# The first two tiles loaded over both DMA queues, split by even and odd partitions

## The chip, the cores and the metric

The kernel runs on one core of a Trainium2 chip. The metric is the device time of one execution, in microseconds. The kernel before was timed in 3 runs, and one further execution was profiled.

## The reference

A gated linear unit on a float32 matrix of 8192 x 8192: the left half of the columns times the sigmoid of the right half. The output is 8192 x 4096.

```python
def reference(x: np.ndarray) -> np.ndarray:
    a, b = np.split(x, 2, axis=-1)
    return a * (1 / (1 + np.exp(-b)))
```

268.4 MB are read and 134.2 MB are written.

## The kernel before

The rows are cut into 32 tiles of 256 rows. A tile has two rows in each of the 128 partitions (`R = 2`), so a partition's share is one run of 64 KiB of the input, its row 0 and its row 1 one behind the other, and 32 KiB of the output. Neighbouring partitions are 128 KiB apart in the input (`h=2` in the rearrangement: two tiles interleave).

There are two input buffers (`xs`, `SLOTS = 2`) and two output buffers (`os`); tile i uses buffer i mod 2. In a tile the columns are counted in eighths, 0 to 4 for the first row and 4 to 8 for the second.

All loads are issued by SyncE (`load`, line 63), all stores by ScalarE (`store`, line 68). Each of the two engines has a DMA queue of its own; on the page the sync queue is q1 and the scalar queue q10. A queue's transfers follow one another, and both queues feed the same 16 DMA engines, which take packets from either. A packet here is one partition's contiguous piece.

The work on a tile (`work`) is: ScalarE takes the sigmoid of the right columns in place (line 92), then VectorE multiplies by the left columns into the output buffer (line 97). In tiles 1 to 30 the sigmoid is one instruction over the tile, and the product is cut into the first 3/16 of the columns (`few`, on GpSimd from tile 2 on, on VectorE in tile 1) and the rest on VectorE. A no-operation on TensorE (line 87) joins the wait for the tile's load and for the store that empties the output buffer. Tiles 0 and 31 are worked in four pieces (`fourths`), each a sigmoid of 128 x 2048 and a product.

Tile 0 is loaded as its two rows, in two transfers, and stored as its two rows; every other load is one transfer of the whole tile, every other store but the last tile's too.

The order is written out at the end of `_tiles`: loads 0 and 1 first; then for each tile its work, the load of tile i + 2 (which waits for the products of tile i, the last readers of that input buffer), and its store. Each instruction keeps its place in the program on its engine. The only waits are those that `place` is given; the others are declared needless because they follow from the ones that are kept.

`_launch_early` takes SyncE's first load out of the body and puts it into the entry block, ahead of the barrier that starts the body, so that it is issued at time 0. `_close_on_sync` rewrites the end: GpSimd clears the semaphores, and SyncE waits for the last store.

Of the kernel before, what the change touches and what calls it, by code (L numbers as in the profile page):

```python
# [8 lines left out]
def _tiles(ctx, tc, x, out):  # L9
    nc = tc.nc  # L10
    P = nc.NUM_PARTITIONS
    DEP = mybir.DependencyInfo(mybir.DependencyClass.Sync, mybir.DependencyReason.DATA)
    fp32 = mybir.dt.float32
    SIG = mybir.ActivationFunctionType.Sigmoid

    n_rows, n_cols = x.shape
    half = n_cols // 2
    R = 2
    SLOTS = 2
    n_tiles = n_rows // (P * R)  # L20
    x_g = x.rearrange("(g p h r) m -> g h p (r m)", p=P, h=2, r=R)
    out_g = out.rearrange("(g p h r) m -> g h p (r m)", p=P, h=2, r=R)

    pool = ctx.enter_context(tc.tile_pool(name="io", bufs=1))
    xs = [pool.tile([P, R * n_cols], fp32, name=f"x_sb{k}") for k in range(SLOTS)]
    os = [pool.tile([P, R * half], fp32, name=f"o_sb{k}") for k in range(SLOTS)]

    whole = [(0, 8)]
    rows = [(0, 4), (4, 8)]
    cut = half // 16 * 3  # L30
    few_and_most = [(0, 8, 0, cut), (0, 8, cut, half)]
    fourths = [(k, k + 2, k % 4 * half // 4, (k % 4 + 2) * half // 4) for k in range(0, 8, 2)]
    loads = [whole] * n_tiles
    works = [few_and_most] * n_tiles
    stores = [whole] * n_tiles
    behind = [0] * n_tiles
    loads[0] = stores[0] = rows
    works[0] = works[-1] = fourths
    stores[-1] = [(0, 4), (4, 6), (6, 8)]
    behind[-1] = 1  # L40

    def meet(a, b):
        return a[0] < b[1] and b[0] < a[1]

    traced = [[] for _ in range(SLOTS)]
    load_of, mul_of, store_of = {}, {}, {}

    def place(i, ins, *needs):


        kept = {n.ins.name for n in needs}
        for e in traced[i % SLOTS]:
            if e.ins.name not in kept:
                tc.declare_no_dep(ins.ins, e.ins, reason="follows from the waits that are kept")
        traced[i % SLOTS].append(ins)
        tc.keep_in_program_order(ins)
        return ins

    def load(i):
        for lo, hi in loads[i]:  # L60
            c = slice(lo * n_cols // 4, hi * n_cols // 4)
            free = [m for w, m in mul_of.get(i - SLOTS, []) if meet(w, (lo, hi))]
            ins = nc.sync.dma_start(out=xs[i % SLOTS][:, c], in_=x_g[i // 2, i % 2, :, c])  # L63
            load_of.setdefault(i, []).append(((lo, hi), place(i, ins, *free)))

    def store(i, lo, hi):
        c = slice(lo * half // 4, hi * half // 4)
        ins = nc.scalar.dma_start(out=out_g[i // 2, i % 2, :, c], in_=os[i % SLOTS][:, c])  # L68
        done = [m for w, m in mul_of[i] if meet(w, (lo, hi))]
        store_of.setdefault(i, []).append(((lo, hi), place(i, ins, *done)))  # L70

    def work(i, lo, hi, near, far):

        rows = xs[i % SLOTS].rearrange("p (r h m) -> p r h m", r=R, h=2)
        packed = os[i % SLOTS].rearrange("p (r m) -> p r m", r=R)
        r, c = slice(lo // 4, (hi + 3) // 4), slice(near, far)
        b = rows[:, r, 1, c]
        landed = [s for w, s in load_of[i] if meet(w, (lo, hi))]
        gone = [s for w, s in store_of.get(i - SLOTS, []) if meet(w, (lo, hi))]
        middle = 0 < i < n_tiles - 1  # L80
        rest = middle and near
        if rest:
            before = mul_of[i].pop()[1]
        else:
            g = rows[:, r, 1, :] if middle else b
            if middle and gone:
                met = nc.tensor.nop(nofuse=True)  # L87
                for n in (*landed, *gone):
                    tc.add_manual_dep(met.ins, n.ins.name, DEP, reason="joins the waits")
                place(i, met, *landed, *gone)  # L90
                landed = [met]
            before = nc.scalar.activation(out=g, in_=g, func=SIG)  # L92
            for n in landed:
                tc.add_manual_dep(before.ins, n.ins.name, DEP, reason="both have landed")
            place(i, before, *landed)
        engine = nc.gpsimd if far == cut and i > 1 else nc.vector
        mul = engine.tensor_mul(out=packed[:, r, c], in0=rows[:, r, 0, c], in1=b)  # L97
        tc.add_manual_dep(mul.ins, before.ins.name, DEP, reason="follows the gate, or the first columns")
        place(i, mul, before, *(() if middle else gone))
        mul_of.setdefault(i, []).append(((lo, hi), mul))  # L100

    for i in range(SLOTS):
        load(i)
    for i in range(n_tiles):
        due = list(stores[i])
        for k, piece in enumerate(works[i]):
            work(i, *piece)
            ready = works[i][k - behind[i]][1] if k >= behind[i] else 0
            while len(stores[i]) > 1 and k < len(works[i]) - 1 and due[0][1] <= ready:
                store(i, *due.pop(0))  # L110
        if i + SLOTS < n_tiles:
            load(i + SLOTS)
        for lo, hi in due:
            store(i, lo, hi)
# [71 lines left out]
@with_exitstack  # L186
def kernel(
    ctx: ExitStack,
    tc: tile.TileContext,
    x: bass.AP,  # L190
    out: bass.AP,
):
    nc = tc.nc
    with ExitStack() as pools:
        _tiles(pools, tc, x, out)
    tc.close()
    tc.compile()
    _launch_early(nc)
    _close_on_sync(nc)
# [30 lines left out]
```

## Time and profile before

| | us |
|---|---|
| median of 3 runs (lowest, highest) | 932.75 (932.47, 932.77) |
| the profiled execution | 932.44 |
| its span, first to last instruction | 931.1 |
| VectorE busy | 232.5 |
| ScalarE busy | 227.0 |
| GpSimd busy | 99.3 |

402.67 MB pass through the 16 DMA engines at a mean of 432 GB/s. The loads take 66.6% of these engines' time, the stores 33.4%. The page's chain of work that ended last is, by share of the span, DMA 69%, VectorE 12%, ScalarE 12% and GpSimd 5%.

How to read these: the span is counted within the profiled execution; what lies around it, 1.34 us, belongs to the time and not to the span. An engine's busy time counts what it computes, not the issuing of DMAs. A row of the timeline or of the chain gives a start and a length in us from the span's start. "ACTq" and "SPq" are the sequencers of ScalarE and SyncE, which issue DMAs. The DMA row of the page gives the mean busy share of the 16 DMA engines in each fortieth of the span, in tenths. "L97" is line 97 of the kernel.

### The profile page before, as it was taken

The numbers are of one execution on the slowest core, as the hardware profiler recorded it, in microseconds if no ns is written. First come the engines' busy times: TensorE is split into PE (matmuls) and PEld (weight loads), VectorE is DVE, ScalarE is ACT, GpSimd is POOL, SyncE is SP. The second block draws the span as 40 slices with busy tenths as digits, with TensorE's granted clock in tenths as the row PEclk, the third lists the DMA queues.
The fourth block names the chain that finished last, engine by engine and source line by source line (L and its number), as shares of the span: only waits on it lengthen the run. The fifth ranks groups of instructions, "written<-read, shape, count | busy, mean of one in ns | idle before, by whom it ended". The sixth has DMA issues, their size and how long they took to land.

```text
span 931.1 us, 299 instructions
## 1 busy us (share of the span) xinstructions
DVE 232.5 (25%) x39; ACT 227.0 (24%) x39; POOL 99.3 (11%) x33
## 2 busy tenths in 40 slices
DVE  1133203332023320233302333023330233311333
ACT  2123332033320333202332023320233202333023
POOL 0001110111101111011110111101111011110110
DMA  9999999999999999999999999999999999999998
GB/s 405 450 442 414 428 450 425 453 405 428 450 428 450 410 469 405 428 450 428 450 405 459 420 428 451 425 450 408 431 448 428 450 408 467 408 428 450 427 452 383
DMA packets 9793, 402.67 MB, mean 432 GB/s; under 512 B 1088, under 2 KB 1088, under 8 KB 1088
## 3 DMA queue, kind: packets, MB, share of 16 engines
q1 hardware_dynamic: 4752, 268.44, 66.6%
q10 hardware_dynamic: 5040, 134.22, 33.4%
q14 instruction: 1, 0.01, 0.0%
HBM read 268.44 MB, written 134.22 MB: 432 GB/s over the span
## 4 chain that ended last, share of the span: by engine, by line
DMA 69%; DVE 12%; ACT 12%; POOL 5%; issue 0%; PEldq 0%; ACTq 0%; SPq 0%
DMA out_dram<-o_sb 60%; DVE o_sb L97 12%; ACT x_sb L92 12%; DMA x_sb<-in_x_dram 9%; POOL o_sb L97 5%; PEldq L87 0%; ACTq L68 0%; SPq L63 0%
## 5 line engine op out<-in xcount | busy, mean ns | idle before, releaser
L97 DVE TENSOR_TENSOR o_sb<-x_sb 128x6656 f32<-128x6656 f32 (+2 forms) x39 | 232.5, 5969 | 690.3 <-POOL o_sb L97 632.7
L92 ACT ACTIVATE x_sb<-x_sb 128x8192 f32<-128x8192 f32 (+1 forms) x38 | 225.7, 5949 | 692.7 <-PEq L87 632.9
L97 POOL TENSOR_TENSOR o_sb<-x_sb 128x1536 f32<-128x1536 f32 x29 | 99.1, 3417 | 793.9 <-ACT x_sb L92 793.9
L92 ACT ACT_TABLE_LOAD x1 | 1.3, 1283 | 0.8 <-PEq L214 0.8
L214 POOL MEMSET const-float32-0.0<- 128x1 f32 x1 | 0.1, 99 | 0.2 <-issue 0.2
L214 POOL MEMSET const-bfloat16-1.0<- 128x1 bf16 x1 | 0.1, 103 | 0.0
L214 POOL MEMSET const-uint8-127<- 128x1 uint8 x1 | 0.1, 103 | 0.0
L214 POOL MEMSET const-float32-1.0<- 128x1 f32 x1 | 0.1, 99 | 0.0
## 6 DMA issues: line engine op xcount, KB each, us to landing
out_dram<-o_sb ACTq DMA_DIRECT2D x30, 4096.0 KB, 40.2
x_sb<-in_x_dram SPq DMA_DIRECT2D x2, 4096.0 KB, 16.6
out_dram<-o_sb ACTq DMA_DIRECT2D x3, 2048.0 KB, 27.8
out_dram<-o_sb ACTq DMA_DIRECT2D x2, 1024.0 KB, 8.3
x_sb<-in_x_dram SPq DMA_DIRECT2D x31, 40.0
```

The lines of the kernel that those rows point to most:

```text
L92: before = nc.scalar.activation(out=g, in_=g, func=SIG)
L97: mul = engine.tensor_mul(out=packed[:, r, c], in0=rows[:, r, 0, c], in1=b)
L214: nc = _bacc.Bacc("TRN2", target_bir_lowering=False, num_devices=1)
```

## The change

Loads 0 and 1 are each split into two transfers: the even partitions on the sync queue, the odd partitions on the scalar queue, each with the partition's whole 64 KiB run. Tile 0 is no longer loaded row by row, and its output is stored in one transfer behind its last product, on the scalar queue. The later loads, the work and all other stores are as before. `by_row` is defined and not used.

```diff
     whole = [(0, 8)]
-    rows = [(0, 4), (4, 8)]
...
-    loads = [whole] * n_tiles
+    every, even, odd = slice(0, P), slice(0, P, 2), slice(1, P, 2)
+    by_parity = [(nc.sync, (0, 8), even), (nc.scalar, (0, 8), odd)]
+    by_row = [(nc.sync, (0, 4), every), (nc.scalar, (4, 8), every)]
+    first_loads = [by_parity, by_parity]
     works = [few_and_most] * n_tiles
     stores = [whole] * n_tiles
     behind = [0] * n_tiles
-    loads[0] = stores[0] = rows
     works[0] = works[-1] = fourths
...
+    def load_over_both(i):
+        for k, (engine, (lo, hi), p) in enumerate(first_loads[i]):
+            c = slice(lo * n_cols // 4, hi * n_cols // 4)
+            ins = engine.dma_start(out=xs[i][p, c], in_=x_g[i // 2, i % 2, p, c])
+            load_of.setdefault(i, []).append(((lo, hi), place(i, ins)))
+
     def load(i):
-        for lo, hi in loads[i]:
-            c = slice(lo * n_cols // 4, hi * n_cols // 4)
-            free = [m for w, m in mul_of.get(i - SLOTS, []) if meet(w, (lo, hi))]
-            ins = nc.sync.dma_start(out=xs[i % SLOTS][:, c], in_=x_g[i // 2, i % 2, :, c])
-            load_of.setdefault(i, []).append(((lo, hi), place(i, ins, *free)))
+        c = slice(0, R * n_cols)
+        free = [m for _, m in mul_of[i - SLOTS]]
+        ins = nc.sync.dma_start(out=xs[i % SLOTS][:, c], in_=x_g[i // 2, i % 2, :, c])
+        load_of.setdefault(i, []).append(((0, 8), place(i, ins, *free)))
...
     for i in range(SLOTS):
-        load(i)
+        load_over_both(i)
```

## The prediction

> **What bounds the kernel now.** I read the page's head, its DMA parts, the windows by stage, the chain that ended last, and the timeline of the first 70 us.
>
> From the page: the span, the DMA busy tenths, the queues (packets, MB, share of 16 engines' time).
>
> ```profile
> span 931.1 us, 299 instructions
> DMA  9999999999999999999999999999999999999998
> q1 hardware_dynamic: 4752, 268.44, 66.6%
> q10 hardware_dynamic: 5040, 134.22, 33.4%
> ```
>
> The windows (stretch, its length, busy time of DVE, ACT, POOL, clock, DMA share, GB/s):
>
> ```profile
> 0.00:46.20 46.20, 8.98 (x4) 8.70 (x5) 0.21 (x4) 1.00 1.02 431
> 99.60:871.60 772.00, 191.47 (x27) 189.78 (x27) 92.26 (x27) 1.00 1.00 434
> ```
>
> The 16 DMA engines have no idle stretch: the loads of the sync queue (q1) and the stores of the scalar queue (q10) add up to 100.0% of their time, and the first 46 us run at 431 GB/s beside 434 in the steady state. VectorE and ScalarE are busy a quarter of it. So only two things change the time: bytes moved more slowly, or engines left without work.
>
> The chain (start, length, what), at both ends of its regular part:
>
> ```profile
> 1.15 45.06 DMA x_sb<-in_x_dram
> 46.23 7.04 ACT x_sb L92
> ...
> 117.35 40.23 DMA out_dram<-o_sb
> ...
> 813.60 40.21 DMA out_dram<-o_sb
> ```
>
> Between 117.35 and 813.60 lie 12 rounds of two tiles: 29.01 us a tile. 32 tiles at that pace are 928.3 us, and the span is 931.1. All that start and end cost above pure transfer is 2.8 us. That is the whole sum that an edit of the start can save from. By the packet records of the trace 0.98 of it passes before the first packet (the first issue, at 0.00, stays where it is) and 0.35 after the last. This leaves under 1.5 us, or 0.16%. About 0.2%, 1.87 us, is what a measurement of this kernel can tell from no change.
>
> The timeline of the start (start, length, engine, what):
>
> ```profile
> 0.77 1.28 ACT L92 ACT_TABLE_LOAD   x1 [0.77 <-PEq L214]
> 12.10 3.71 ACT L92 ACTIVATE x_sb<-x_sb 128x2048 f32<-128x2048 f32 x2 [10.04 <-DMA x_sb<-in_x_dram]
> 14.04 4.49 DVE L97 TENSOR_TENSOR o_sb<-x_sb 128x2048 f32<-128x2048 f32 x2 [14.04 <-ACT x_sb L92]
> 18.57 0.38 ACTq L68 DMA_DIRECT2D out_dram<-o_sb  x1
> ...
> 28.28 34.25 SPq L63 DMA_DIRECT2D x_sb<-in_x_dram  x2
> 28.28 0.36 ACTq L68 DMA_DIRECT2D out_dram<-o_sb  x1
> 46.23 7.03 ACT L92 ACTIVATE x_sb<-x_sb 128x8192 f32<-128x8192 f32 x1 [20.70 <-DMA x_sb<-in_x_dram]
> ```
>
> Tile 0 comes in two halves (12.10, 21.82), its two stores go out at 18.57 and 28.28 and share the engines with the load of tile 1, which is why that lands only at 46.2.
>
> **The change, part by part.** The listing of the changed program shows where each instruction goes.
>
> *Packets.* Per DMA engine, tile 0's load goes from 16 packets of 32 KiB (1.213 us each in the packet records) to 8 of 64 KiB (2.418): 8 x (2 x 1.213 - 2.418) = 0.06 us saved. Tile 0's store goes from 16 of 16 KiB (0.611) to 8 of 32 KiB: 16 x 0.611 - 8 x 1.213 = 0.07 saved. Tile 1's load keeps its packets. Together -0.13 us, on the path, since the engines are the bound. The total of DMAs stays 68, so their closing words cancel.
>
> *First packets.* The first 16 packets took 1.55 to 2.15 us instead of 1.213, 0.65 more on the mean; the first packets of tile 1, behind the change of size, took 0.14 too long on the mean. Nothing in this trace shows two queues both loading. Bounds: the 0.14 disappears and nothing follows (-0.14), or the scalar queue's first packets pay a first-packet cost of their own (+0.65). I take 0: in the steady part a q10 packet between two q1 packets takes no longer than its norm.
>
> *Issues.* SyncE issues two loads instead of three (0.33 us each). ScalarE issues two (0.36 us each by its store rows) from 0.77 on, so its queue is filled by about 1.5 us, and its packets can follow by about 2.5, behind the first 64 KiB packet that lasts until 4. Cost 0; without that cover 1 us at most.
>
> *The activation table.* In the listing it now stands behind ScalarE's two issues and waits for the odd partitions' semaphore, so 1.28 us move from 0.77 to behind tile 0's landing. Counted next.
>
> *Tile 0 as a whole.* With the two queues alternating it is 8 packets per engine: 0.98 + 0.65 + 8 x 2.415 = 20.95, landed about 21.2. Then 1.3 for the table, 1.94 for the first gate and 4 products at 2.25 behind it: finished at about 33.4, against 28.28 now. Two things wait for that: load 2 on SyncE (behind it load 3, which waits for tile 1 anyway) and store 0 on ScalarE (behind it tile 1's gate, which waits for tile 1's landing). Cover: tiles 0 and 1 keep the engines busy for 16 packets, until 0.98 + 0.65 + 16 x 2.415 = 40.3. An issue's first packet came 0.98 after the issue, so load 2 is in its queue by about 34.4, 5.9 us before it is needed. Cost 0; without the cover, each us late costs one.
>
> *Tile 1.* No store shares its time, so it lands at about 40.4 rather than 46.2. Its work (7.04 + 1.77 + 7.10) ends at 56.4 and puts load 3 and store 1 into the queues, while load 2 and store 0 last until 40.3 + 29.0 = 69.3. By 69.3 the engines have moved loads 0 to 2 and store 0, as they have by about 70 now. From here on the two programs are alike, down to the last store. The 5.8 us by which tile 1 is earlier are no gain: the stores that were in its way are only moved behind it.
>
> *Rate of a half.* The rows above are of 128-partition transfers. None in this trace has 64 partitions with a step of two. Bounds: the same 2.42 us for a 64 KiB packet (nearest row: the same size, the same partitions), or, if pairs of engines meet at one place in SBUF, twice that. I take the same: the even and odd partitions together are exactly the rows moved now. [...]
>
> **Sum.** 931.1 - 0.13, with -0.14 to +0.65: 930.8 to 931.6, likeliest 931.0. The profiled execution took 932.44 in all, 1.34 outside the span, and stands 0.31 below the median of 932.75. So 932.3 for such an execution, and 932.6 as a median: no change that can be measured.
>
> **Rivals.**
>
> [...]
>
> 2. *The queues do not alternate at the start* (slower). If q1 goes through all its 8 packets first, tile 0 lands after 12 packets, at 30.8; its work ends at 43.0, load 2 flows from 44.0, and the engines are empty for 3.7 us: 936. It costs from a landing after 27.1 us on. Against it: between loads and stores the packets alternate one by one from 23.6 us on.
>
> 3. *The start's excess goes* (faster). If two queues hide the first packets' cost and every later one, up to the 1.5 us above are won: 931.2, still within 0.2%. To gain more, the packets themselves would have to move faster than 434 GB/s, which no long stretch of the trace shows.
>
> That the change does not do what it says is hardly open: the listing has two 64x16384 loads on each queue and one whole store of tile 0.
>
> **How the numbers follow.** Forecast 0.76; rival 1 0.09; rival 2 0.03; something at the start that no row shows, of 2 us or more, 0.04; rival 3 0.08, of which 0.02 for over 0.2%. So faster 0.02, same 0.76 + 0.06 = 0.82, slower 0.16. The range runs from rival 3's end (931.3) to the forecast with its dearest start (+0.65 and 0.13 not saved, 933.5), plus 0.7 for a mild form of the slower ones: 934.2. What is left out above it is most of the 0.16.
>
> **What would show it.** Right: 64 KiB packets of q1 and q10 alternating from about 4 us at 2.42 us each; tile 0's first gate at about 22.5, behind a table load; load 2 and store 0 issued near 33.4; tile 1's gate near 40.4; DMA share near 1.00 in every window up to 70; rounds of 58.0 us after that; an end alike. Wrong: under 425 GB/s between 2 and 40 us (rival 1), tile 0 landing after 27 us or a DMA hole near 41 us (rival 2), or a span that does not fit 32 tiles at 29.01 us plus 2.8.

## The result, and the profile after

The changed kernel takes 954.08 us (median of 4 runs, 953.39 to 955.05) where the kernel before takes 932.61: a ratio of 1.0231, interval 1.0218 to 1.0244. It is 21 us slower, and the forecast was no change. Ratios here compare undisturbed executions; of four experiments below the executions spread by per cents, and for these the whole range is given.

The page of the changed kernel, the lines that answer to those of before:

```profile
span 952.0 us, 299 instructions
DMA  9999999999999999999999999999999999999998
q1 hardware_dynamic: 4480, 260.05, 65.0%
q10 hardware_dynamic: 5056, 142.61, 34.7%
```

The DMA engines are as full as before. The bytes are the same, with 8.4 MB moved from q1 to q10, and they take 21 us longer. So no hole opened: transfers became slower. The windows of the changed kernel say where:

```profile
46.20:99.60 53.40, 15.94 (x3) 11.83 (x2) 3.42 (x1) 1.00 1.00 432
99.60:871.60 772.00, 184.40 (x26) 182.76 (x26) 88.80 (x26) 1.00 1.00 425
```

The second stretch is the one that the change does not touch. It ran at 434 GB/s before and runs at 425 now, with the DMA share at 1.00 in both. The chain of the changed kernel shows the same (start, length, what):

```profile
59.95 43.33 DMA out_dram<-o_sb
121.07 41.66 DMA out_dram<-o_sb
...
834.00 41.31 DMA out_dram<-o_sb
```

From 121.07 to 834.00 it makes 12 rounds of two tiles, 59.4 us each, where before it was 58.0. Load 2 ends at 69.7 in both kernels by the packet records (the mean over the 16 engines). Load 31 ends at 928.5 instead of 910.9: 29.62 us a tile instead of 29.01, over 29 tiles 17.7 us. The rest of the span, 23.5 us behind load 31 instead of 20.2, makes up the other 3.3.

The packet records give each packet's queue, start, length and size. Strung together by where one ends and the next starts, they show a DMA engine's order of work. L is a 64 KiB load packet, S a 32 KiB store packet, l and s the 4-byte word that closes a load or a store; lengths in us; around 450 us:

```
before   L 2.418  S 1.213  l  s  L 2.418  S 1.213  L 2.418  S 1.213
changed  L 2.418  S 1.213  l  S 1.213  L 2.418  s  L 2.585  S 1.213  L 2.862  S 1.213  L 2.418
```

In these records an engine takes one item from each queue in turn: from 100 to 870 us 99% of the steps from one item to the next change the queue, in both kernels. Before, a load and the store beside it end in the same turn, and their words stand together (446.82 and 446.83 us on the mean of the 16 engines). In the changed kernel the store queue is one turn late (423.60 and 427.23): the load's word uses up q1's turn, so two store packets follow one another, and then the store's word uses up q10's turn, so two load packets do. Some of the next three load packets are longer, up to 3.6 us, in every tile. Nearly all other packets of the steady part have their old lengths (of the store packets from 100 to 870 us 99.7% are at 1.21 us). On the mean of the 16 engines, all the load packets together are 19.2 us over their norm, against 1.0 before. The engines also drift apart: the 16 closing words of a load lie within 0.4 to 0.6 us before, and spread from 0.6 us at load 0 to 5.3 at load 24 in the changed kernel.

The timeline of its start:

```profile
1.20 1.37 ACTq L63 DMA_DIRECT2D x_sb<-in_x_dram  x2
19.84 1.28 ACT L98 ACT_TABLE_LOAD   x1 [19.84 <-DMA x_sb<-in_x_dram]
24.64 7.31 ACT L98 ACTIVATE x_sb<-x_sb 128x2048 f32<-128x2048 f32 x4 [3.52 <-DMA x_sb<-in_x_dram]
...
35.51 0.37 ACTq L74 DMA_DIRECT2D out_dram<-o_sb  x1
43.97 7.03 ACT L98 ACTIVATE x_sb<-x_sb 128x8192 f32<-128x8192 f32 x1 [12.02 <-DMA x_sb<-in_x_dram]
```

The scalar queue's first packets begin at 6.8 us, behind two of the sync queue's (1.33 and 4.4). So q10 ends its halves of tiles 0 and 1 later, and store 0 starts one turn behind load 2. Both queues have the next transfer waiting when one ends (from load 3 on, a load is issued 2.2 to 9.5 us ahead of the first closing word of the load that is running, a store together with it), so this stays: up to 660 us all 16 engines are one turn late. Later some come level again, without becoming faster: from 760 to 900 us three engines have the two words side by side in every tile, and their load packets are 0.66 to 0.87 us a tile over the norm, beside 0.59 to 0.76 on the ten that stay one turn late. By then an engine's own order does not tell whether it is slow.

### The profile page after: what moved, and what is told of

Read it like the earlier page. It is cut to its first block, busy times and chain, and to the rows that moved or that the text cites. A ratio compares the mean times of both kernels' runs of the same rounds, so it can differ in the third digit from the quotient of the medians.

```text
span 952.0 us, 299 instructions
## 1 busy us (share of the span) xinstructions
DVE 232.4 (24%) x39; ACT 226.9 (24%) x39; POOL 99.3 (10%) x33
## 2 busy tenths in 40 slices
DMA packets 9537, 402.67 MB, mean 423 GB/s; under 512 B 1088, under 2 KB 1088, under 8 KB 1088
## 4 chain that ended last, share of the span: by engine, by line
DMA 70%; DVE 12%; ACT 11%; POOL 5%; issue 0%; ACTq 0%; PEldq 0%
DMA out_dram<-o_sb 61%; DVE o_sb L103 12%; ACT x_sb L98 11%; DMA x_sb<-in_x_dram 8%; POOL o_sb L103 5%; PEldq L93 0%; ACTq L63 0%; ACTq L74 0%
## 6 DMA issues: line engine op xcount, KB each, us to landing
out_dram<-o_sb ACTq DMA_DIRECT2D x31, 4096.0 KB, 41.6
```

## The experiments

Theory A: the one turn that the store queue is behind, set in the first microseconds, is the whole loss. Theory B: the loading over both queues does it in another way. The tool of most runs is a transfer that is cut into its even and its odd partitions on its own queue. It moves the same packets and needs one more closing word on each engine (both traces have 1088 words for 68 transfers, 16 each), so its queue should fall back by one turn:

```diff
+        for p in (slice(0, P, 2), slice(1, P, 2)) if i in SPLIT_LOADS else (slice(0, P),):
+            ins = nc.sync.dma_start(out=xs[i % SLOTS][p, c], in_=x_g[i // 2, i % 2, p, c])
```

(and the same for `SPLIT_STORES` on the scalar queue).

**1. Level the queues in the changed kernel.**

```diff
+    SPLIT_LOADS, SPLIT_STORES = (2,), ()
```

> The changed kernel with one edit: load 2 is issued as two transfers on the sync queue, even and odd partitions, so that queue spends one more closing word (one more turn) before load 3. Theory A (lag): in the changed kernel the store queue runs one turn behind the load queue from tile 2 to the end, the closing words of a load and of the store beside it no longer come together, and each tile costs 0.2 to 0.9 us for it; one extra turn on the sync queue puts them level again, so every later tile takes 29.0 us and the time is 932.6 + about 1.4 (dearer start) = 934, at most 936. Theory B (the split loads at the start leave the 16 DMA engines out of step with one another, whatever the order of the queues): the loss stays, 952 to 956.

Measured: 933.45 us, ratio to before 1.0008 (0.9999 to 1.0018). The loss is gone, with everything at the start left in place. The windows of this run:

```profile
128.00:273.00 145.00, 35.46 (x5) 35.15 (x5) 17.08 (x5) 1.00 1.00 434
650.00:795.00 145.00, 35.46 (x5) 35.15 (x5) 17.08 (x5) 1.00 1.00 434
```

**2. Make the store queue late in the kernel before.**

```diff
+    SPLIT_LOADS, SPLIT_STORES = (), (8,)
```

> The kernel before with one edit: store 8 is issued as two transfers on the scalar queue, even and odd partitions, so that the store queue spends one more turn and falls one turn behind from there on. Nothing at the start is changed. Theory A (lag): 29.0 us a tile up to tile 10 and then the excess that the changed kernel has in its first 22 tiles, 12 us in sum: 945, between 940 and 949. Theory B (it is the start): 932.7, since the start is that of before.

Measured: 947.56 us, ratio 1.016 (1.0143 to 1.0177). Its windows, one ahead of store 8 and two behind it:

```profile
128.00:273.00 145.00, 35.47 (x5) 35.15 (x5) 17.08 (x5) 1.00 1.00 433
331.00:476.00 145.00, 35.46 (x5) 35.15 (x5) 17.08 (x5) 1.00 1.01 428
650.00:795.00 145.00, 33.00 (x5) 35.15 (x5) 17.08 (x5) 1.00 1.01 426
```

The start of before, and the loss of the changed kernel from tile 10 on. As there, it grows: load 10 to load 11 took 29.2 us, later ones 29.6.

**3. Cut a load and the store beside it** (`(10,), (8,)` in the kernel before).

> The kernel before with load 10 and store 8, which share the engines, each issued as two transfers, even and odd partitions: both queues spend one more turn and stay level. Theory A (lag): no more than 0.3 us over before, 932.6 to 933.0. Rival C (a 64-partition transfer in the steady part disturbs the engines by itself): as the run with store 8 alone split, about 945.

Measured: 932.68 us, ratio 0.9999 (0.999 to 1.0008). Transfers of 64 partitions cost nothing that this run shows; what run 2 lost came with the shift.

**4. Make the load queue late** (`(10,), ()`).

> The kernel before with load 10 alone issued as two transfers on the sync queue, so that from there on it is the load queue that is one turn behind. Theory A1 (what costs is two loads in a row, where a store's closing word takes a turn between them): with the load queue behind, the packets still alternate one by one, load, store's word, load's word, store: 932.6 to 933.0. Theory A2 (any shift costs, once the two closing words are not at the same boundary): about 12 us as in the run with store 8 alone, 940 to 949.

Measured: 933.16 us, ratio 1.0005 (0.9995 to 1.0014). One turn late on the load side was free here.

**5. The store part of the change alone.**

```diff
-    loads[0] = stores[0] = rows
+    loads[0] = rows
```

> The kernel before with the store part of the change alone: tile 0 is stored whole, its load stays in two halves on the sync queue. Theory A (lag): the whole store is issued at about 28.3, in the middle of load 1, so the store queue starts some four turns early and runs ahead of the load queue; the two closing words do not come together, a store's word stands between two load packets in every tile, and the tiles take 29.2 to 29.9 us: 944 to 955. Rival D (the doubled loading alone is the cause): 932.7.

Measured: 934.39 us, ratio 1.002 (1.001 to 1.0029). The expectation was wrong by 9.6 us or more, in an instructive way. Near 430 us an engine's order is `L s L S L S l S L`: two loads in a row, a store's word between them, in every tile, and each load packet at 2.418. Tiles take 29.0 us. So it is not two loads in a row that cost. Here the store queue runs ahead of the load queue.

**6. The load part alone** (tile 0 stored as its two rows).

```diff
+    stores[0] = [(0, 4), (4, 8)]
```

> The changed kernel with the store part undone: tile 0 is stored as its two rows, each in 16 KiB packets. Theory A (lag): the two row stores take 18 turns where the whole one takes 9, so store 0 ends only with load 3, at about 90 us; tile 2's work, which needs that output buffer, ends at about 108, the engines have only store 1 left from 90 to 100 and stand idle for some 9 us until load 4; then load 4 and store 2 start together, level, and the tiles take 29.0 us: 941 to 946, with a hole near 100 to 109. Rival D (the loads over both queues set the slow state whatever the store does): 950 to 956 with slow tiles to the end.

Measured: 944.95 us, ratio 1.013 (1.0113 to 1.0147), by another way than the whole change. Its windows:

```profile
60.00:90.00 30.00, 0.00 (x0) 0.00 (x0) 0.00 (x0) 1.00 1.00 434
100.00:110.00 10.00, 7.09 (x1) 0.64 (x1) 1.79 (x1) 1.00 0.19 52
139.00:168.00 29.00, 7.09 (x1) 7.03 (x1) 3.42 (x1) 1.00 1.00 434
```

The row stores keep output buffer 0 until 90 us, the engines stand idle from about 100 to 110, and behind the hole the queues start level and keep 434 GB/s. So the loads over both queues do not force the slow tiles; whether they appear depends on how the stores fall in behind.

**7. Two turns late on the load side** (`(10, 12), ()` in the kernel before).

> The kernel before with loads 10 and 12 both issued as two transfers on the sync queue, so that the load queue is two turns behind from tile 12 on. Theory A1 (two loads in a row, with a store's word between them, cost): one turn behind was free because the two words still came side by side; with two turns a store's word stands between two load packets again, and the rest of the run has the excess of the run with store 8 split in its first 19 tiles, 10 us: 943, between 939 and 947. Theory A3 (only a late store queue costs, a late load queue is free): 933.0 to 934.

Measured: 933.27 us, ratio 1.0007 (0.9998 to 1.0017). Order `L s L S l S L`, all at their norms. With run 5 this rules out A1, that two loads in a row cost.

**8. Take away the head start** (the changed kernel).

```diff
-    _launch_early(nc)
```

> The changed kernel without the early launch of the sync queue's first load, so that both queues are filled from about 0.8 us on. Theory A (lag from the head start): in the changed kernel the sync queue's packets have two turns before the scalar queue's first; without the head start it should be one, the halves of tiles 0 and 1 end level, and the time is 933.4 plus the 0.8 us of the later start: 933.5 to 935. If two packets still go first, the theory gives the changed kernel's 954 to 956. Theory B (the loading over both queues itself): 954 to 956 in either case.

Measured: 934.28 us, ratio 1.0017 (1.0008 to 1.0026). Its timeline and windows:

```profile
0.73 1.19 SPq L63 DMA_DIRECT2D x_sb<-in_x_dram  x2
0.75 1.45 ACTq L63 DMA_DIRECT2D x_sb<-in_x_dram  x2
```

```profile
2.00:40.00 38.00, 8.90 (x4) 8.59 (x5) 0.00 (x0) 1.00 1.04 442
331.00:476.00 145.00, 35.46 (x5) 35.15 (x5) 17.09 (x5) 1.00 1.00 434
```

In its packet records the queues alternate from the first packet on, and all pairs of words stand together. Starting the sync queue 0.7 us later (the scalar queue's first issue is 0.45 us earlier here) makes the changed kernel 20 us faster.

**9 and 10. Two and three turns late on the store side** (`(), (8, 10)` and `(), (8, 10, 12)` in the kernel before).

> The kernel before with stores 8 and 10 both issued as two transfers, so that the store queue is one turn behind from tile 10 and two turns behind from tile 12 on. Theory P (any late store queue costs): as with store 8 alone, 943 to 950. Theory Q (only one turn costs, where a store's word falls right behind the first packet of the next load): the excess ends with tile 12, 933.0 to 936.

> The same with stores 8, 10 and 12, three turns behind from tile 14 on. Theory P (any late store queue costs): 943 to 950. Theory Q (only one turn costs): the excess ends with tile 12, 933.0 to 936.

Measured: run 9 from 933.02 to 954.28 us over 10 executions, median 941.22; run 10 from 933.35 to 955.12, median 940.49. Neither theory said this. The profiled execution of run 9 (933.02) has slow packets only in the two tiles that are one turn late; from then on the order is `l S L S L s L S`, at the norms. In that of run 10 (939.97) three turns do not last: from 445 us on 15 engines are two turns late and one is one turn late, and the tiles take 29.0 us up to 790. From 500 to 780 us the load packets of that one engine are 0.28 us a tile over the norm, those of the 15 others 0.03 or less: within one trace, an engine that is one turn late is slower than its neighbours that are two.

**11. Other distances in HBM** (run 2 with the rows of a tile laid next to one another).

```diff
-    x_g = x.rearrange("(g p h r) m -> g h p (r m)", p=P, h=2, r=R)
+    x_g = x.rearrange("(g h p r) m -> g h p (r m)", p=P, h=2, r=R)
...
```

(and the same for `out_g`).

> The run with store 8 split (store queue one turn behind), with the rows of a tile laid next to one another: neighbouring partitions are 64 KiB apart in the input and 32 KiB in the output, instead of 128 and 64. Theory H (the excess is a meeting of the 16 engines' streams in HBM, which depends on the distance of their rows): the excess changes by more than half, to under 940 or over 955. Otherwise (the order of turns alone): as before, 945 to 950.

Measured: 947.45 us, ratio 1.0157 (1.0142 to 1.0172), as run 2. Halving the distance between the partitions' rows, from 128 to 64 KiB in the input, changed nothing (947.56 us in run 2).

**12. Little work on the tiles** (the changed kernel).

```diff
+    works[2:] = [[(0, 8, 0, cut), (0, 8, cut, cut + half // 8)]] * (n_tiles - 2)
-            g = rows[:, r, 1, :] if middle else b
+            g = rows[:, r, 1, : half // 8 if i > 1 else half] if middle else b
```

> The changed kernel with little work on tiles 2 to 30: the sigmoid over an eighth of the columns, the products over three sixteenths and an eighth (the rest of these outputs is left as it was). The sigmoid of 7.0 us starts with the store's word and lies over just the two or three load packets that are slow. Theory E (the engines' SBUF traffic slows the DMA there): 932.6 + about 1.5 = 933.5 to 936. Theory A (the order of turns alone): 950 to 957 as the changed kernel, with the load and the store issued some 10 us earlier.

Measured: 953.33 us, ratio 1.0219 (1.0204 to 1.0234). The rest of the outputs of tiles 2 to 30 is left out. A window of the changed kernel, and the same of this run:

```profile
331.00:476.00 145.00, 34.02 (x5) 35.15 (x5) 17.08 (x5) 1.00 1.00 423
```

```profile
331.00:476.00 145.00, 6.12 (x5) 5.28 (x5) 17.08 (x5) 1.00 1.00 425
```

ScalarE and VectorE do about a sixth of the work (GpSimd as much as before) and the DMA is as slow. Nor does it matter here that the next load and store are issued some 12 us earlier.

**13 and 14. Two turns late at once**: the kernel before with store 8 in three transfers, and the changed kernel with store 0 in two.

```diff
+        for p in (slice(0, P, 2), slice(1, P, 4), slice(3, P, 4)) if i in SPLIT_STORES else (slice(0, P),):
```

> The kernel before with store 8 issued as three transfers (even partitions, and the odd ones in two quarters), so that the store queue goes from level to two turns behind at once, without the stage of one turn in between. Theory Q (only one turn behind costs): 932.8 to 934 in every execution. Theory P (any late store queue costs): 943 to 950. If executions spread from 933 to 954 as with stores 8 and 10 split, two turns behind is itself unstable.

> The changed kernel with store 0 issued as two transfers, even and odd partitions: the store queue, one turn behind in the changed kernel, is two turns behind from tile 2 on. Theory Q (only one turn behind costs): 933.4 to 935 in every execution, a repair by adding to the queue that is already late. Theory P (any late store queue costs): 950 to 957.

Measured: run 13 has eight executions between 932.49 and 932.81 and two at 935.08 and 939.64; run 14 has six between 933.28 and 935.86 and six between 951.58 and 957.99. Neither theory gives both; it is the unstable case that the expectation of run 13 names. The profiled execution of run 14 (951.95) has both in one trace:

```profile
128.00:273.00 145.00, 35.46 (x5) 35.15 (x5) 17.08 (x5) 1.00 1.00 433
331.00:476.00 145.00, 35.46 (x5) 35.15 (x5) 17.09 (x5) 1.00 0.99 427
650.00:795.00 145.00, 32.70 (x5) 35.15 (x5) 16.37 (x5) 1.00 0.99 412
```

A turn of a load and a store packet is 3.6 us. In the packet records the store's closing word comes 7.3 us behind the load's, two turns, up to 360 us, and the tiles take 29.0. At 390 us it comes 5.0 behind, at 420 us 3.9 on the mean, with 15 of the 16 engines at one turn, and from there the tiles take 29.4 to 31.4. So two turns late was free in this run while it lasted, up to 360 us, and slipped to one. One turn does not stay either: from about 600 us on 10 to 13 of the 16 engines have the two words side by side, as in the kernel before, and the tiles still take 29.8 us or more, with the load packets of these engines 0.9 to 1.1 us a tile over the norm (700 to 880 us). What still differs from the kernel before is that three to six engines are not level, and that all are out of step with one another: a load's closing words spread over 2.3 to 6.9 us.

The traces also show how two turns slip. Here a late store holds up the work on the next tile and with it the issue of the next load. In the kernel before, the next load is issued 10.3 us ahead of the first closing word of the load that is running; with two turns it is 2.8 to 3.3 (profiled executions of runs 9 and 13, which hold). In run 14 it is 2.4 for the issue at 356 us and 1.9 for the one at 385, and there at least 13 engines take a second store packet at the load queue's turn (`l S S L s`). In run 10 all 16 do so behind the issue at 413 us, with 1.6. These engines ended their load 1.6 to 2.4 us after the next one's issue. This is read from four traces; no run varies it.

No version beats the kernel before: the best repaired one is run 1, at 1.0008.

## Why the prediction was wrong

*The bound* was right: 16 engines without idle time, and a gain at the start of no more than 1.5 us.

*Packets, issues, the table.* The first packet of the change came at 1.33 instead of 0.98, and the first 16 were 0.83 us over their norm instead of 0.65. The table load stood at 19.84, not behind the whole tile: by its time, what it waited for was the half that landed first, the sync queue's and not the scalar queue's. Hidden, as forecast. Tile 0's gate began at 24.64 (forecast 22.5), load 2 and store 0 were issued at 35.5 (33.4), tile 1's gate began at 43.97 (40.4), and load 2 was through at 69.7 (69.3). These delays were covered, with no hole in the DMA row.

*Rate of a half* was right. No run shows the slower packets, up to twice 2.42 us, that the chance of 0.09 for rival 1 stood for: the even and odd halves move at 2.418 us a packet from the second packet on, and run 8 moves load 1, in transfers of 64 partitions alone, from 22.3 to 41.6 us: 8.39 MB at 434 GB/s. The sign that the prediction gave for this rival, under 425 GB/s between 2 and 40 us, did appear in the changed kernel:

```profile
2.00:40.00 38.00, 8.90 (x4) 8.59 (x5) 0.00 (x0) 1.00 0.96 414
```

It misleads. A window counts the packets that start in it, and the first 16 start at 1.33 to 1.58 us, ahead of it; in run 8 they start at 2.07 and later, are counted, and make the 442 above.

*The second rival* had the place right and the price wrong. The queues did not alternate from the first packet; two packets of q1 went first, not eight. I priced only a hole near 41 us, and there was none.

*The step that failed* is "From here on the two programs are alike, down to the last store", the steady part at a price of 0. It looked only at bytes and at whether work was queued; "their closing words cancel" counted the words as time (9 ns each) and not as turns. It took 29.0 us a tile for a property of the DMA engines, when it is also one of the order in which the two queues' transfers end (29.62 with the stores one turn late). That order was in the trace of before: the words of load 2 and of the store beside it came at 69.7 both, and so in every later tile. Measured, the steady part cost 17.7 us, and the end 3.3 with engines out of step. Runs 1 and 8 take this out of the changed kernel and run 2 puts it into the kernel before. That a store queue one turn late sets off the loss is shown. Without the shift (run 1) the change costs 0.8 us, which is not clear of noise and inside the forecast range. Why the load packets lengthen is open, and so is why they stay long on engines that are level again (changed kernel, run 14); a rival that no run separates is that the engines, once out of step with one another, hold each other up (one engine alone out of step did not, run 10). The runs exclude two loads in a row (5, 7), the distance of rows in HBM as far as it was changed (11), most of the work of ScalarE and VectorE (12) and the 64-partition transfers (3).

## What to carry to other kernels

Here two queues kept the DMA engines full, and the position of one against the other, set by first packets at 1.33 and 6.8 us, lasted on all 16 engines up to 660 us. So an edit of the first microseconds is to be judged by the pace of the steady part as well: compare when a load and the store beside it land. Stores that ended one packet turn behind their loads cost 1.6 to 2.3% here (run 2, the changed kernel), and one transfer cut in two put it right (run 1, ratio 1.0008). A full DMA row said that the engines were busy, not that they moved bytes at their best (434 and 425 GB/s from 99.6 to 871.6 us, under the same row): read the GB/s of the stretch that the change does not touch.

## What the runs showed of the hardware

- With both queues backlogged, loads in 64 KiB and stores in 32 KiB packets ran at 433 to 434 GB/s where on all 16 engines the stores ended in the same turn as the loads (before, runs 1 and 8), ahead of them (5) or with the loads one or two turns behind (4, 7), and at 423 to 428 where the stores were one turn behind (changed kernel, 2, 11). In run 14, with the engines out of step, being level again on 10 to 13 of them did not bring the rate back (412 from 650 to 795 us).
- A closing word of 4 bytes took 9 ns and its queue's turn, as a packet does (in the changed kernel the store's word comes 3.63 us behind the load's around 425 us, beside 3.63 for one load and one store packet). One transfer more on the store queue, with no more bytes, cost 15 us (run 2), one more on each queue nothing (run 3, ratio 0.9999).
- Where an engine's load ended 1.6 to 2.4 us after the next load's issue, the store queue got the load queue's next turn (run 10 at 413 us, run 14 at 385); where the first closing word came 2.8 to 3.3 us after it, none was lost (9, 13).
- In the changed kernel the load packet at 43 us, just ahead of the first store packet behind loads alone, took 3.32 to 3.49 us on the 16 engines instead of 2.42.
